# Running the chunked RWKV-7 recurrence on chunk transition matrices formed for eight chunks at a time

## The chip, the cores and the metric

The kernel runs on 1 core of one Trainium2 chip. The metric is the device time of one execution in microseconds (us), given as the median of several runs. One profiled execution, with its trace, is what the views below are read from.

## The reference

The reference is one layer of a hybrid encoder for 1024 tokens of width 1024: a projection of the normed input, three groups of heads on its columns (attention on a memory, a convolution module, a bidirectional RWKV-7 time mixing), an output projection, and a mixture of 16 experts, in float32. What matters here is the time mixing, 6 heads of 64, run forward and backward:

```python
def wkv7_scan(r, w, k, v, kk, a, reverse):
    def step(state, inp):
        r_t, w_t, k_t, v_t, kk_t, a_t = inp
        sa = jnp.einsum('bhij,bhj->bhi', state, -kk_t)
        state = (state * w_t[..., None, :]
                 + sa[..., :, None] * (kk_t * a_t)[..., None, :]
                 + v_t[..., :, None] * k_t[..., None, :])
        y_t = jnp.einsum('bhij,bhj->bhi', state, r_t)
        return state, y_t
    ...
    _, ys = lax.scan(step, state0, (r, w, k, v, kk, a), reverse=reverse)
```

## The kernel before

The scan is cut into chunks of C = 64 tokens. Two heads sit in the 128 partitions (`lo` and `hi`, 64 each), both directions d = 0, 1 go along together, and eight chunks (HC) make a unit, so there are six units u = 0 to 5: three pairs of heads, two halves of the sequence each. For each unit these generators run:

- `prep` (L775) forms, per direction, the decayed vectors: AR (from kk and r) and BK (from k and kk*a). BK is kept with zeros in the half of the partitions that belongs to the other head, so that a product over all 128 partitions is right; three VectorE operations and one of GpSimd of 64 partitions by 512 fill it (L823 to L826).
- `within` (L845) multiplies BK by AR inside each chunk (32 products of 128x128x128) and masks the result into AM with eight VectorE operations (L857).
- `invert` (L887) inverts the 64x64 triangles of all chunks of a unit at once: ScalarE copies blocks of AM into Ld (L895), VectorE turns them into Lt (L900), 31 dependent steps of two VectorE operations follow (L910, L911), then two turns, two scalings, and two rounds of small products with ScalarE copies (L926 to L949) give TT. Ld, Lt, Dt and their successors have one buffer each, so `invert` of the next unit starts when that of this one is through.
- `prep2` (L860) turns BK into BT and v into the first half of SV.
- `chain` (L954) is the recurrence. For a chunk it does, for both directions together: X = AM times v plus AR times the state (L969, L971), a VectorE copy to Xs (L973), SA = TT times Xs (L981), a VectorE and a ScalarE copy of the halves into SV (L982, L983), S1 = BT times SV (L988), and two VectorE operations that scale S1 and add the decayed old state `sps`, which GpSimd made (L991, L965). The outputs Y take two more products (L976, L996). A chunk is three steps of the generator, a unit 24.

The order of the work is written out by a planner: `run` (L224) steps through the chains as `mains`, and beside step i it steps other generators (`fills`) in proportion between two given steps: `within`, `inv`, `prep2` and `prep` of later units, `residual` (L1067, the output projection of the first five blocks, with its operands loaded from DRAM into one buffer each, `fo`), `finish`, and at the end `swap`, `out56` (L1176) and `partial` (L1168). Needs between them (name, count) force a generator to be stepped first. So `within` of unit u waits for steps 12 and 24 of chain u-2, `inv` for step 24 of chain u-2 and for `inv` of u-1, and chain u needs `inv` and `prep2` of u. Each engine runs its instructions in the order that comes out of this. After the chains the last normalisation, the router and the experts follow.

Of the kernel before, what the change touches and what calls it, by code (L numbers as in the profile page):

```python
# [20 lines left out]
P = 128  # L21
# [46 lines left out]
R_P1 = [26, 46]  # L68
# [3 lines left out]
R_W = [1, 2]  # L72
R_P2 = [4, 14]
R_INV = [-4, 22]
R_P = [4, 16]
R_PP = [-10, 8]
# [24 lines left out]
def hybrid_block_kernel(ctx: ExitStack, tc: tile.TileContext, x, xT, memT, memn, w_in, w_mk, w_mv, pcols,  # L101
# [47 lines left out]
    V.memset(bd64[64:128, 64:128], 1.0 / C)  # L149

# [503 lines left out]
    def early():  # L654
# [10 lines left out]

        Z["BK"] = [ge.tile([P, HC, 2, 2, C], F32, name=f"BK{d}") for d in range(2)]
        for bk in Z["BK"]:
            G.memset(bk[hi, :, 0], 0.0)
            G.memset(bk[lo, :, 1], 0.0)
# [13 lines left out]
    def late():  # L683
# [8 lines left out]
        for nm, shape in (("AR", [P, 2, HC, 2, C]), ("BT", [P, 2, HC, 2, C]), ("SV", [P, 2, HC, 2, C])):  # L692
            Z[nm + "b"] = gl.tile(shape, F32, name=nm + "b")
        g2 = pool("g2", stack=ph2b)
        for nm, shape in (("AR", [P, 2, HC, 2, C]), ("BT", [P, 2, HC, 2, C]), ("SV", [P, 2, HC, 2, C])):
            Z.setdefault(nm, []).append(g2.tile(shape, F32, name=nm + "a"))
            Z[nm].append(Z.pop(nm + "b"))
# [77 lines left out]
    def prep(p, k, g):  # L775
# [7 lines left out]
        for d in range(2):  # L783
# [60 lines left out]

    def within(g):  # L845

        for q, d in ((0, 0), (0, 1), (1, 0), (1, 1)):
            AM = g["AM", d, q] = Z["AM"][g["u"] % 2 * 4 + q * 2 + d]
            for h in range(2):
                ps = mm("A", shape=[P, 4, 2, C], name="psA", bufs=2)  # L850
                r_ = slice(h * 64, h * 64 + 64)
                for c in range(4):
                    cc = q * 4 + c
                    T.matmul(ps[:, c].rearrange("p a b -> p (a b)"),  # L854
                             lhsT=g["BK", d][:, cc, h].rearrange("p a b -> p (a b)"),
                             rhs=g["AR"][:, d, cc].rearrange("p a b -> p (a b)"), start=True, stop=True)
                V.tensor_tensor(AM[:, :, h], ps, mask[:, None].to_broadcast([P, 4, 2, C]), op=ALU.mult)  # L857
                yield

    def prep2(p, k, g):  # L860
        BT = g["BT"] = Z["BT"][g["u"] % 2]
        SV = g["SV"] = Z["SV"][g["u"] % 2]
        for d in range(2):
            n = k if d == 0 else 1 - k

            for h in range(2):
                ps = mm(shape=[P, HC, C])
                r_ = slice(h * 64, h * 64 + 64)
# [771 lines left out]
```

## Time and profile before

| | |
|---|---|
| median of 3 runs | 1480.16 us (1478.07 to 1490.92) |
| profiled execution: its own time | 1489.13 us |
| profiled execution: its span | 1487.2 us |
| mean granted TensorE clock | 0.927 |
| busy in the span: PE (TensorE matmul) | 1333.4 us, 90% |
| busy in the span: DVE (VectorE) | 1216.1 us, 82% |
| busy in the span: ACT (ScalarE) | 831.2 us, 56% |
| busy in the span: POOL (GpSimd) | 266.4 us, 18% |

How to read it: times are from the start of the span. Matmuls are pipelined, so a busy PE is not a PE at its peak. The chains run from about 381 to 802 us, the experts from about 880 us to the end. The shares above are means over stages with different limits, so the stage of the chains has to be looked at by itself.

### The profile page before, as it was taken

The numbers are of one execution on the slowest core, as the hardware profiler recorded it, in microseconds if no ns is written. First come the engines' busy times: TensorE is split into PE (matmuls) and PEld (weight loads), VectorE is DVE, ScalarE is ACT, GpSimd is POOL, SyncE is SP. The second block draws the span as 40 slices with busy tenths as digits, with TensorE's granted clock in tenths as the row PEclk, the third lists the DMA queues.
The fourth block names the chain that finished last, engine by engine and source line by source line (L and its number), as shares of the span: only waits on it lengthen the run. The fifth ranks groups of instructions, "written<-read, shape, count | busy, mean of one in ns | idle before, by whom it ended". The sixth has DMA issues, their size and how long they took to land.

```text
span 1487.2 us, 24329 instructions
## 1 busy us (share of the span) xinstructions
PE 1333.4 (90%) x9238; PEld 1069.4 (72%) x9238; DVE 1216.1 (82%) x2120; ACT 831.2 (56%) x1214; POOL 266.4 (18%) x238
## 2 busy tenths in 40 slices
PE   6888999997888889888999719999999999999996
PEld 5777667675777776767868618888888887887773
DVE  8899975699686869696833678999999988998886
ACT  4222574433535244434322418888888877887875
POOL 2233322532120312130221000100000110110010
PEclk9999899998898888888999859999999999999998
DMA  8212112422443533342473657999999999999985
GB/s 294 71 61 67 64 64 97 152 71 73 141 143 93 157 97 117 105 121 84 142 272 142 269 198 293 386 393 390 385 385 390 381 379 344 370 377 377 370 302 201
DMA packets 146100, 327.91 MB, mean 220 GB/s; under 512 B 9792, under 2 KB 64960, under 8 KB 145984
## 3 DMA queue, kind: packets, MB, share of 16 engines
q1 hardware_dynamic: 139360, 303.14, 55.6%
q0 software_dynamic: 6192, 22.55, 5.4%
q8 instruction: 72, 1.18, 0.3%
q10 hardware_dynamic: 432, 0.68, 0.1%
q14 instruction: 44, 0.36, 0.1%
HBM read 288.58 MB, written 37.75 MB: 219 GB/s over the span
## 4 chain that ended last, share of the span: by engine, by line
PE 60%; DVE 23%; DMA 6%; ACT 5%; issue 4%; POOL 1%; SPq 0%; POOLq 0%; DVEq 0%; ACTq 0%
PE mm L330 14%; PE mm L331 14%; PE mm L329 14%; DVE cv L517 3%; DVE dtmp L910 2%; DVE Dt L911 2%; DMA fo<-oT_d 2%; PE mm L1435 2%; ACT Ld L895 2%; DMA xk<-in_xT_dram 1%; PE mm L745 1%; PE psA L854 1%; DVE ewl L1354 1%; PE mm L1165 1%; PE mm L1575 1%
## 5 line engine op out<-in xcount | busy, mean ns | idle before, releaser
L1354 DVE SCALAR_TENSOR_TENSOR ewl<-eraw,pc,ewh 128x1024 fp32r<-128x1024 f32 x256 | 315.6, 1280 | 30.5 <-ACT ewh L1353 28.4
L1353 ACT ACTIVATE ewh<-eraw,pc 128x1024 fp32r<-128x1024 f32 x256 | 283.8, 1149 | 31.7 <-PE mm L331 25.7
L330 PE MATMUL mm<-ewl,xh 128*128 128x512 f32 x512 | 202.1, 395 | 3.2 <-DVE ewl L1354 3.0
L331 PE MATMUL mm<-ewh,xl 128*128 128x512 f32 x512 | 200.1, 391 | 0.0
L329 PE MATMUL mm<-ewh,xh 128*128 128x512 f32 x512 | 190.4, 397 | 2.5 <-ACT ewh L1353 2.5
L1350 DVE TENSOR_TENSOR ewl<-eraw,ewh 128x1024 fp32r<-128x1024 f32 x120 | 139.0, 1219 | 2.8 <-ACT ewh L1349 2.8
L329 PE MATMUL mm<-hh,wh 128*128 128x512 f32 x304 | 125.4, 413 | 9.6 <-ACT hh L310 9.6
L1349 ACT ACTIVATE ewh<-eraw 128x1024 fp32r<-128x1024 f32 x120 | 121.6, 1057 | 10.6 <-PE mm L331 9.5
L331 PE MATMUL mm<-hh,wl 128*128 128x512 f32 x304 | 125.5, 413 | 0.8 <-POOL wl L325 0.8
L330 PE MATMUL mm<-hl,wh 128*128 128x512 f32 x304 | 125.1, 412 | 0.9 <-DVE hl L311 0.9
L330 PEld LDWEIGHTS mm<-ewl,xh 128*128 128x128 f32 x512 | 96.6, 189 | 25.8 <-DVE ewl L1354 7.3
L329 PEld LDWEIGHTS mm<-ewh,xh 128*128 128x128 f32 x512 | 96.1, 188 | 23.2 <-ACT ewh L1353 4.2
L331 PEld LDWEIGHTS mm<-ewh,xl 128*128 128x128 f32 x512 | 96.3, 188 | 19.7 <-DVE xl L1438 0.2
L330 PE MATMUL mm<-ewl,fh 128*128 128x512 f32 x240 | 94.6, 394 | 0.3 <-DVE ewl L1350 0.2
L331 PE MATMUL mm<-ewh,fl 128*128 128x512 f32 x240 | 93.6, 390 | 0.0
L329 PE MATMUL mm<-ewh,fh 128*128 128x512 f32 x240 | 88.0, 390 | 0.0
L325 POOL TENSOR_TENSOR wl<-wraw,wh 128x512 fp32r<-128x512 f32 x38 | 58.7, 1548 | 124.5 <-ACT wh L324 83.6
L329 PEld LDWEIGHTS mm<-hh,wh 128*128 128x128 f32 x304 | 59.6, 196 | 25.4 <-ACT hh L310 9.6
L1472 POOL DMA_INDIRECT x_d<-ye,idx x15 | 25.9, 1724 | 283.3 <-ACT ye L1471 283.3
L1420 POOL DMA_INDIRECT xe<-h_d,idx x16 | 28.9, 1805 | 247.0 <-DVE gates L1418 182.3
L517 DVE SCALAR_TENSOR_TENSOR cv<-u,cw,cv 128x512 f32<-128x512 f32 (+1 forms) x87 | 71.5, 853 | 0.1
L330 PEld LDWEIGHTS mm<-hl,wh 128*128 128x128 f32 x304 | 59.1, 194 | 17.4 <-issue 2.7
(417 smaller groups left out, 2950.7 us busy)
## 6 DMA issues: line engine op xcount, KB each, us to landing
eraw<-in_w_eg_dram SPq DMA_DIRECT2D x64, 1024.0 KB, 7.9
eraw<-in_w_eu_dram SPq DMA_DIRECT2D x64, 1024.0 KB, 9.1
eraw<-in_w_ed_dram SPq DMA_DIRECT2D x64, 1024.0 KB, 7.4
fo<-oT_d SPq DMA_DIRECT2D x64, 320.0 KB, 3.9
wraw<-in_w_in_dram SPq DMA_DIRECT2D x38, 256.0 KB, 2.8
ld_k<-d_k SPq DMA_DIRECT2D x18, 256.0 KB, 3.1
ld_v<-d_v SPq DMA_DIRECT2D x18, 256.0 KB, 3.3
xk<-in_xT_dram SPq DMA_DIRECT2D x16, 256.0 KB, 4.7
```

Source lines behind the costliest of these rows:

```text
L325: G.tensor_sub(wl, raw, wh.bitcast(F32))
L329: T.matmul(ps, lhsT=lh, rhs=rh, start=first, stop=False)
L330: T.matmul(ps, lhsT=lh, rhs=rl, start=False, stop=False)
L331: T.matmul(ps, lhsT=ll, rhs=rh, start=False, stop=last)
L517: V.scalar_tensor_tensor(o[:, 0:ln], z, w, o[:, 0:ln], op0=ALU.mult, op1=ALU.add)
L895: A.copy(Ld[r_, :, c:c + 4].rearrange("p t c -> p c t"), g["AM", d, q][r_, :, h, 0, b * 32:b * 32 + 32])
L910: IE.tensor_tensor(tmp[:, sg, ts], lcol, drow, op=ALU.mult)
L911: IE.tensor_tensor(Dt[:, sg, ts], Dt[:, sg, ts], tmp[:, sg, ts], op=ALU.add)
L1349: A.activation(h, raw[a], AF.Copy)
L1350: V.tensor_sub(l, raw[a], h.bitcast(F32))
L1353: A.activation(h, raw[a], AF.Copy, scale=gain)
L1354: V.scalar_tensor_tensor(l, raw[a], gain, h.bitcast(F32), op0=ALU.mult, op1=ALU.subtract)
```

## The change

The state over a chunk is S1 = M S0 + own, with M = I plus a product that doesn't depend on the state. A new generator `solve` forms, for the eight chunks of a unit and both directions, M and the transposed output factor (both into AR) and the own part of the state (into the second half of BT), and the own corrections U (into the second half of SV). `chain` then does for a chunk the product M S0 on top of the own part, one VectorE operation that scales it, and the products of the outputs, which are put behind. `sps`, Xs, SA and the copies into SV are gone. BK loses its zeroed halves, so `within` and `prep2` use products of 64 partitions. The places of the fills and their needs are new. Two explicit orders (`edge`) keep products of different row halves that write one PSUM bank apart.

```diff
-R_P1 = [26, 46]
+R_P1 = [24, 33]
-R_W = [1, 2]
-R_P2 = [4, 14]
-R_INV = [-4, 22]
+R_W = [-10, -4]
+R_P2 = [0, 10]
+R_INV = [-7, 16]
+R_S = [11, 23]
+R_1 = {"within": [8, 12], "inv": [9, 20], "prep2": [9, 14], "solve": [17, 24]}
+R_S0 = [19, 23]
...
-            V.tensor_mul(BK[lo, :, 0, 0, :], kd[lo], cl[lo])
-            (G, V)[FL[7]].tensor_mul(BK[hi, :, 1, 1, :], kd[hi], cl[hi])
-            for r_, h, i in ((lo, 0, 1), (hi, 1, 0)):
-                V.scalar_tensor_tensor(BK[r_, :, h, i, :], sg[r_], -0.5, cl[r_], op0=ALU.mult, op1=ALU.mult)
+            V.tensor_mul(BK[:, :, 0, :], kd, cl)
+            V.scalar_tensor_tensor(BK[:, :, 1, :], sg, -0.5, cl, op0=ALU.mult, op1=ALU.mult)
...
+    HR = ((0, lo, hi), (1, hi, lo))
     def within(g):
...
+            for c in range(4):
+                cc = q * 4 + c
+                for i in range(2):
+                    for h, r_, w_ in HR:
+                        T.matmul(ps[h][w_ if i else r_, c].rearrange("p a b -> p (a b)"),
+                                 lhsT=g["BK", d][r_, cc, i], rhs=g["AR"][r_, d, cc].rearrange("p a b -> p (a b)"),
+                                 start=True, stop=True)
...
+    def solve(g):
+        AR, SV, BT = g["AR"], g["SV"], g["BT"]
+        U = SV[:, 1]
+        def each(tagp, f):
+            ps = mm(tagp, shape=[P, HC, C], name="psU")
+            for cc in range(HC):
+                for h, r_, w_ in HR:
+                    o, l, r = f(cc, h, r_, w_)
+                    T.matmul(ps[o, cc], lhsT=l, rhs=r, start=True, stop=True)
+            return ps
...
+        for d in range(2):
+            ps = each("mm", lambda cc, h, r_, w_: (w_, am(d, r_, cc, h, 0), SV[r_, 0, d, cc]))
+            A.copy(U[:, d], ps)
+            yield
+            ps = each("A", lambda cc, h, r_, w_: (w_, AR[r_, d, cc, 0, :], ident[r_, r_]))
+            A.copy(AR[:, d, :, 0, :], ps)
+            yield
+        TT = g["TT"].rearrange("p (d c) a b -> p d c (a b)", d=2)
+        for d in range(2):
+            ps = each("mm", lambda cc, h, r_, w_: (w_, TT[w_, d, cc], U[w_, d, cc]))
+            A.copy(U[:, d], ps)
+            yield
+            ps = each("A", lambda cc, h, r_, w_: (w_, TT[w_, d, cc], AR[w_, d, cc, 0, :]))
+            A.copy(AR[:, d, :, 0, :], ps)
+            yield
+        for d in range(2):
+            pm_ = each("mm", lambda cc, h, r_, w_: (r_, AR[w_, d, cc, 0, :], BT[w_, 1, d, cc]))
+            pr_ = each("A", lambda cc, h, r_, w_: (r_, AR[w_, d, cc, 0, :], am(d, w_, cc, h, 1)))
+            V.tensor_tensor(AR[:, d, :, 0, :], pm_, id2[:, None].to_broadcast([P, HC, C]), op=ALU.add)
+            yield
+            V.tensor_tensor(AR[:, d, :, 1, :], AR[:, d, :, 1, :], pr_, op=ALU.add)
+            yield
+        for d in range(2):
+            ps = each("mm", lambda cc, h, r_, w_: (r_, BT[w_, 1, d, cc], U[w_, d, cc]))
+            A.copy(BT[:, 1, d], ps)
             yield
...
+        def own(cc):
+            S1 = mm("cx", shape=[P, 2, C], name="psS", bufs=2)
+            for d in range(2):
+                for r_ in (lo, hi):
+                    T.matmul(S1[r_, d], lhsT=ident[r_, r_], rhs=BT[r_, 1, d, cc], start=(d == 0), stop=False)
+            for d in range(2):
+                for r_ in (lo, hi):
+                    T.matmul(S1[r_, d], lhsT=BT[r_, 0, d, cc], rhs=SV[r_, 0, d, cc], start=False, stop=False)
+            return S1
...
+        S1, St = own(0), []
         for cc in range(HC):
             S0 = state[0]
...
+            ms = [T.matmul(S1[r_, d], lhsT=AR[r_, d, cc, 0, :], rhs=S0[r_, d], start=False, stop=(d == 1)).ins
+                  for d in range(2) for r_ in (lo, hi)]
+            Sn = Z["sp"].tile([P, 2, C], F32, name="S0", bufs=4)
+            op = V.tensor_tensor(Sn, S1, pcs[:, :, cc:cc + 1].to_broadcast([P, 2, C]), op=ALU.mult)
             state[0] = Sn
+            if cc + 1 < HC:
+                S1 = own(cc + 1)
+            if cc == 0:
+                others = out_own(0, 1) + out_own(1, 1)
+            else:
...
+                    edge(lead, op.ins, mybir.DependencyClass.Sync)
...
+            for _ in range(3):
+                yield
...
+             "solve0": (solve(gs[0]), 14, *R_S0, [(0, "within0", None), (0, "prep20", None), (4, "inv0", None)]),
...
-        needs = [(1, f"inv{u}", None), (0, f"prep2{u}", None)]
+        needs = [(0, f"solve{u}", None)]
...
+            fills[f"within{u}"] = (within(gs[u]), 8, *at_(R_W if u > 1 else R_1["within"], u - 1), [(0, f"prep{u}", None), *after(u - 2, 0, 4)])
...
-            mains["swap"] = (swap(), 1, [(0, n, None) for n in ("res", "bon2", "pp2", "prep5", "within5", "inv5", "prep25")])
+            mains["swap"] = (swap(), 1, [(0, n, None) for n in ("res", "bon2", "pp2", "prep5", "within5", "solve5")])
```

In the parts left out `prep2` writes BT as two halves for both heads with 64x64 products against the identity (in place of transposes) and one full copy of v into SV; `out_own` and `out_state` hold the products of the outputs; `inv` of unit u waits for the first step of chain u-2, `prep2` for its step 19; chain S0 has four buffers.

## Rows read from the trace of the kernel before

**Rows 1.** Busy us (count) of PE, PEld, DVE, ACT, POOL; PEclk; DMA: stretches of `invert`.

```profile
316.40:355.20 38.80, 37.81 (x158) 29.23 (x156) 36.77 (x82) 8.25 (x10) 7.08 (x7) 1.00 0.11 41
398.30:456.60 58.30, 51.63 (x617) 43.36 (x617) 49.77 (x132) 17.57 (x34) 11.49 (x12) 0.91 0.46 136
470.40:529.50 59.10, 52.87 (x585) 43.02 (x586) 49.03 (x125) 17.92 (x34) 13.58 (x14) 0.79 0.42 127
529.50:546.90 17.40, 16.17 (x237) 13.70 (x237) 7.93 (x22) 10.99 (x24) 1.67 (x2) 0.83 0.24 70
546.90:610.90 64.00, 56.98 (x595) 45.62 (x594) 56.80 (x166) 22.81 (x43) 16.64 (x17) 0.81 0.39 118
628.80:680.90 52.10, 44.21 (x556) 34.87 (x548) 48.82 (x125) 17.18 (x35) 13.26 (x14) 0.90 0.40 119
696.40:736.90 40.50, 38.17 (x468) 32.63 (x468) 34.66 (x119) 11.16 (x21) 7.27 (x9) 0.84 0.47 141
747.90:840.00 92.10, 88.36 (x795) 71.59 (x794) 36.44 (x95) 23.06 (x45) 14.67 (x22) 0.93 0.53 206
```

**Rows 2.** Chain of waits from 456.6 to 747.9 us, shares by line.

```profile
by line: DVE dtmp L910 7.6%; DVE Dt L911 7.2%; DMA fo<-oT_d 7.0%; ACT Ld L895 6.1%; issue 4.7%; PE mm L329 4.3%; PE mm L331 3.9%; PE psS L988 3.4%; PE mm L745 3.3%; PE mm L330 3.2%; PE psA L854 2.9%; DMA fraw<-in_w_out_dram 2.4%; DVE BK L82
```

**Rows 3.** Timeline around one pause of `invert`, VectorE: start us, us, operation.

```profile
529.52 0.70 DVE L926 STREAM_TRANSPOSE D<-TT 128x512 f32<-128x512 f32 x1
...
546.89 1.24 DVE L900 STREAM_TRANSPOSE Lt<-Ld 128x1024 f32<-128x1024 f32 x1
```

**Rows 4.** Timeline in the same pause, ScalarE.

```profile
536.23 1.16 ACT L949 COPY TT<-mm 32x512 f32<-32x512 f32 x2 [0.85 <-PE mm L945]
...
538.95 3.34 ACT L895 COPY Ld<-AM 32x128 f32<-32x128 f32 x8
```

**Rows 5.** Groups by shape, 381 to 840 us: count | busy us, mean ns | idle before.

```profile
L895 ACT COPY Ld<-AM 32x128 f32<-32x128 f32 x80 | 32.4, 405 | 5.2 <-DVE AM L857 4.2
L857 DVE TENSOR_TENSOR AM<-psA,mask 128x512 f32<-128x512 f32 x39 | 26.6, 685 | 4.9 <-PE psA L854 4.5
...
L991 DVE SCALAR_TENSOR_TENSOR S<-psS,pcs,sps 128x64 f32<-128x64 f32 x96 | 24.7, 278 | 18.2 <-PE psS L988 17.7
...
L854 PE MATMUL psA<-ARb,BK 128*128 128x128 f32 x128 | 21.0, 299 | 2.0 <-DVE BK L826 1.6 <-DVE Dt L911 0.4
...
L973 DVE COPY Xs<-psX 128x128 f32<-128x128 f32 x48 | 13.7, 286 | 17.0 <-PE psX L971 15.6 <-PE psY L976 1.3
...
L826 DVE SCALAR_TENSOR_TENSOR BK<-sg,cl 64x512 f32<-64x512 f32 x16 | 12.4, 778 | 0.2
...
L823 DVE TENSOR_TENSOR BK<-ta,cl 64x512 f32<-64x512 f32 x9 | 9.1, 1012 | 0.0
...
L982 DVE COPY SVb<-psSA 64x128 f32<-64x128 f32 x24 | 7.1, 294 | 7.5 <-PE psSA L981 7.1
L871 ACT COPY BTb<-mm 128x512 f32<-128x512 f32 x12 | 7.0, 579 | 6.8 <-PE mm L870 6.8
```

**Rows 6.** Timeline of TensorE in one chunk of the last chain.

```profile
762.55 0.27 PE L976 MATMUL psY<-ARb,S 64*64 64x64 f32 x2
...
762.62 0.23 PE L971 MATMUL psX<-S,ARb 64*64 64x64 f32 x2
...
763.30 0.45 PE L981 MATMUL psSA<-Xs,TT 64*64 64x64 f32 x8 [0.30 <-DVE Xs L973]
763.68 0.49 PE L329 MATMUL mm<-wo,oh 128*128 128x512 f32 x1
```

**Rows 7.** Timeline of VectorE and GpSimd side by side in the third chain.

```profile
563.99 0.40 POOL L965 TENSOR_TENSOR sps<-S,pcs 128x128 f32<-128x128 f32 x1 [4.71 <-DVE S L991]
564.14 0.39 DVE L910 TENSOR_TENSOR dtmp<-Lt,Dt 128x120 f32<-128x120 f32 x1
...
571.42 1.27 POOL L824 TENSOR_TENSOR BK<-ta,cl 64x512 f32<-64x512 f32 x1 [7.03 <-DVE ta L819]
571.46 1.78 DVE L823 TENSOR_TENSOR BK<-ta,cl 64x512 f32<-64x512 f32 x1
```

More of the change, by code (lines that the diff above doesn't have):

```diff
@@ L664, in early @@
         Z["TT"] = [ge.tile([P, NCH, 2, 32], F32, name="TT0")]
[L666 to L669, printed above, removed]
+        Z["BK"] = [ge.tile([P, HC, 2, C], F32, name=f"BK{d}") for d in range(2)]
         Z["ep"] = ge.tile([P, HC, C + 1], F32, name="ep")
@@ L848, in within @@
             AM = g["AM", d, q] = Z["AM"][g["u"] % 2 * 4 + q * 2 + d]
-            for h in range(2):
[L850 to L857, printed above, removed]
+            ps = [mm("A", shape=[P, 4, 2, C], name="psA", bufs=2) for _ in range(2)]
+            for c in range(4):
[5 more added lines that the diff above has]
+                                 start=True, stop=True)
+            for h in range(2):
+                V.tensor_tensor(AM[:, :, h], ps[h], mask[:, None].to_broadcast([P, 4, 2, C]), op=ALU.mult)
                 yield
@@ new lines, in edge, with out_own @@
+        def edge(ins, other, cls):
+            tc.add_manual_dep(ins, other.name, mybir.DependencyInfo(cls, mybir.DependencyReason.DATA),
+                              reason="row tiles of one bank")
+        def out_own(d, i):
+            return [T.matmul(Y[d][r_, cc], lhsT=SV[w_ if i else r_, i, d, cc],
+                             rhs=g["AM", d, cc // 4][w_ if i else r_, cc % 4, h, 1, :],
+                             start=(i == 1 and cc == 0), stop=False).ins for cc in range(HC) for h, r_, w_ in HR]
@@ L966, in chain @@
-            X = mm("cx", shape=[P, 2, C], name="psX", bufs=2)
-            for d in range(2):
-                for h, r_, w_ in ((0, lo, hi), (1, hi, lo)):
-                    T.matmul(X[w_, d], lhsT=AM[d][r_, c4, h, 0, :], rhs=SV[r_, d, cc, h, :], start=True, stop=False)
-                for r_, w_ in ((lo, hi), (hi, lo)):
-                    T.matmul(X[w_, d], lhsT=AR[r_, d, cc, 0, :], rhs=S0[r_, d], start=False, stop=True)
-            Xs = Z["sp"].tile([P, 2, C], F32, name="Xs", bufs=2)
-            (A.copy if FL[3] else V.tensor_copy)(Xs, X)
@@ L974, in chain @@
-            for d in range(2):
-                for r_ in (lo, hi):
-                    T.matmul(Y[d][r_, cc], lhsT=S0[r_, d], rhs=AR[r_, d, cc, 1, :], start=True, stop=False)
-            yield
-            SA = mm("cx", shape=[P, 2, C], name="psSA", bufs=2)
-            for d in range(2):
-                for r_ in (hi, lo):
-                    T.matmul(SA[r_, d], lhsT=TT[r_, d, cc], rhs=Xs[r_, d], start=True, stop=True)
-            (A.copy if FL[4] else V.tensor_copy)(SV[hi, :, cc, 0, :], SA[hi])
@@ L983, in chain @@
-            (V.tensor_copy if FL[5] else A.copy)(SV[lo, :, cc, 1, :], SA[lo])
-            yield
-            S1 = mm("cx", shape=[P, 2, C], name="psS", bufs=2)
-            for d in range(2):
-                for h, r_ in ((0, lo), (1, hi)):
-                    T.matmul(S1[r_, d], lhsT=BT[:, d, cc, h, :], rhs=SV[:, d, cc, h, :], start=True, stop=True)
-            Sn = Z["sp"].tile([P, 2, C], F32, name="S0", bufs=3)
-            for d in range(2):
-                V.scalar_tensor_tensor(Sn[:, d], S1[:, d], pcs[:, d, cc:cc + 1], sps[:, d], op0=ALU.mult,
-                                       op1=ALU.add)
@@ L993, in chain @@
[L993 to L997 removed]
+            St.append(S0)
+            ms = [T.matmul(S1[r_, d], lhsT=AR[r_, d, cc, 0, :], rhs=S0[r_, d], start=False, stop=(d == 1)).ins
+                  for d in range(2) for r_ in (lo, hi)]
+            Sn = Z["sp"].tile([P, 2, C], F32, name="S0", bufs=4)
```

55 lines of the change are left out of this document (33 added, 22 removed).

## The prediction

> **What bounds the kernel now.** The page says PE 90% and DVE 82% busy, but these are means over the whole span, and the change touches only the stage of the chains (381 to 802 us) and the 38 us of leftovers behind it. I looked for what paces a unit there. In the chain of waits of that stage no line holds more than 8%: it hops between the two operations of an inversion step, the loads of `fo`, the copies to Ld, and matmuls [rows 2]. So I cut the stage at the two turns of `invert` that come once a unit, Lt and D. Between them lies a stretch in which 31 dependent steps run on VectorE; between D and the next Lt lies a pause [rows 3]. The stretches of units 1 to 5 take 58.3, 59.1, 64.0, 52.1 and 40.5 us, 274.0 in all, with VectorE busy for 239.1 of them, 87% [rows 1]. The pauses between the ends shown are 13.8, 17.4, 17.9 and 15.5 us, and 11.0 from the last D to 747.9, where TT of unit 5 is ready: 75.6 in all; VectorE is busy for 7.9 of the 17.4 in the pause shown. `invert` has one set of buffers, so stretch and pause follow each other strictly, and their sum, 350 us, is the stage. VectorE paces the stretches. The pause is a relay: D at 529.5, TT copied by 537.4, sixteen copies to Ld (0.405 us each, 6.5 in all [rows 5]) until Lt at 546.9 [rows 3, 4]. After 747.9 come 92.1 us in which PE is busy for 88.4 and VectorE for 36.4 [rows 1]: there TensorE is the bound.
>
> **The stretches.** The recurrence costs VectorE 13.7 us in Xs, 24.7 in the state, and twice 7.1 in SA (two buffers of SV, one shown): 52.6 for six units, 8.8 a unit [rows 5]. It becomes one operation a chunk from PSUM of 128x128. No row shows it; the Xs copy of that shape takes 0.286 us, the two halves of the state together 0.556. I take the first, since it is one instruction over the same elements: 2.3 us a unit, 4.4 at the other end, so 6.5 saved (4.4 at least). The stretches are 78% of the 350 us, so 5.1 of it falls into each, 25 us in five. BK costs VectorE one operation of 1.012 and two of 0.778 us a direction; it becomes two of full height, which I put at the 0.685 of the masked copy, the row of 128x512 [rows 5]: 2 x (2.57 - 1.37) = 2.4 a unit, for units 2 to 5, whose `prep` lies here, 9.6. `solve` adds four operations of 128x512 from PSUM, 4 x 0.685 = 2.7 a unit; its place is the second half of the chain before, half of which I put into the stretch: 1.4 x 5 = 7 (0 to 14). VectorE is relieved of 25 + 9.6 - 7 = 28 us; at 87% busy that is 32 us of time.
>
> The other part is idle time of VectorE, 35 us in the stretches. It stands at the head of its queue for Xs 17.0 us, for the state 18.2 and for SA 7.5 and more, 43 in 381 to 840 [rows 5], with the inversion steps queued behind each time. Three such hand-overs a chunk become one, with TensorE; but a queue that skips one wait meets the next (`fo` holds 7% of the chain of waits [rows 2]). I count 13 of the 35 us. Stretches: -45 (-20 if no wait goes and VectorE's added work all lies here, -60 if half of the idle goes too).
>
> GpSimd loses `sps` and its part of BK. The row where VectorE's part of BK lies beside GpSimd's shows 1.78 us, and a step beside `sps` its usual 0.39 [rows 7]; the mean of 1.012 above holds the first already. The Trainium skill, SBUF - State Buffer, section "Who interferes with whom", says that a VectorE operation with two SBUF inputs and a GpSimd operation that reads SBUF lock each other out whole, whoever starts first; the first pair agrees, the second shows no delay of VectorE. By that rule alone the eight `sps` of a unit, 0.4 us each, would give back up to 3 us more a unit, 16 in five; the sum goes by the rows.
>
> **The pauses.** Both halves of the relay stay, 7.9 and 6.5 us. `within` now runs a chain ahead, so no mask has to be waited for (the longer pauses hold some 3 us more than the relay). Against that, `solve` puts ten ScalarE copies of 128x512 into ScalarE's queue, 0.579 us each [rows 5], 5.8 a unit, and Ld's copies may stand behind them. 0 in all (-15 to +25).
>
> **TensorE.** A chain's own products stay 192 a unit. `prep2` splits each of its transposes into two products for the two halves of the rows, nothing in sum. `within` goes from 32 products of 128 rows to 64 of 64 rows. `solve` adds 224 products, 112 pairs. A pair alone takes 0.23 us, four pairs 0.45 [rows 6], so 0.07 each: 8 us a unit at the full clock (PEclk 1.00, 2.4 GHz), 16 where it is at 1.2. The stretches were granted 0.79 to 0.91, means of the two levels [rows 1]. In them PE shows busy 85 to 94%, which would leave no room; but a product of L854 lasts 0.299 us by its row, while 128 of them made PE busy for 21.0 us, 0.164 each [rows 5], so that a good part of "busy" is the tail of a pipeline that other products fill. I count nothing for it in the stretches, and the full 8 as a rival. Products of different quadrants run side by side (Y beside X [rows 6]), which would halve `within`, 5.2 us a unit; not counted. The Trainium skill, TensorEngine Tiling (Array Packing), section "Key Properties", says that a change of tiling mode drains TensorE. That speaks against 14 more bursts a unit of small products between the wide ones of `residual`. The last small burst starts at 763.30, ends at 763.75, and the wide product behind it starts at 763.68 [rows 6]: no drain longer than the last product's own length. The rule names no time; at the length of one small pair, 0.23 us, for each of two changes a burst, 14 bursts would cost 6 us a unit more, and rival (3) would be dearer by that.
>
> **Both ends.** `solve` now stands between `invert` and its chain. Where another inversion follows, VectorE has its stretch to run meanwhile; it is bare before chain 0 and for unit 5. Ten evacuations come behind TT, each a burst of 8 pairs (0.6 us) and a copy of 0.58 or an operation of 0.69, 1.2 us; the two directions overlap: 6 to 12 us. Before chain 0 `prep` of unit 1 can run beside it: +5 (0 to 12). For unit 5 the last chain and `swap`, and with it all of `out56`, wait: +10 (6 to 17). Behind it the 92.1 us of TensorE's work stay but for the idle 3.7 and some of the eight chunks' starts: -6 (-12 to 0).
>
> Sum: -45 + 0 + 5 + 10 - 6 = -36 on the profiled execution's 1489.1 us, 1453. That execution is 0.6% above the median; the same ratio on 1480.2 gives **1444 us**.
>
> **The rivals.** (1) VectorE gets so free that the stretches fall to the pace of those with no chain's hand-overs or little else in them, 38.8 us (unit 0) and 40.5 (unit 5) [rows 1]: 43 in the four middle ones saves 61, pauses of 12 us another 15: -61 - 15 + 15 - 6 = -67, 1413. For it: these two stretches exist. Against it: unit 0's had 95% of VectorE and no `finish` or `prep` beside it. (2) The gain is eaten: no idle goes (-20), each pause takes 4 of the 5.8 us of ScalarE's copies (+20), and the ends take +9: +9, 1489, and with half of the copies hidden -1, 1479. For it: the loads of `fo` have one buffer each and hold 7% already, and the step per chunk isn't short where own parts and outputs stand before it in TensorE's queue. Against it: the stretches are where VectorE is fullest. (3) Slower: TensorE is the bound in the stretches after all. Then VectorE's relief is worth nothing, and each unit pays 8 us (6 if `within` gets cheaper): 6 x 8 = 48 and the bare solves 15 less 6, +57, 1537; it is slower by over 1% from 1 us a unit on. For it: PE is busy 94% in the last stretch, and at least as much as VectorE in three others. Against it: the pipelined count above, and VectorE's idle time before the chain's operations, in which the products came late behind other work, not for want of TensorE's time alone. (4) That the change doesn't do what it says, a state over a chunk in one product and one operation, is not a case by itself: the code leaves it no other path; late products are in (2).
>
> **How the numbers follow.** Forecast 0.5, (1) 0.2, (2) 0.2, (3) 0.1. The range leaves out (3) and the far halves of (1) and (2), so 1405 to 1475. One per cent, 15 us, is about what a measurement of this kernel can tell from no change: faster than 1465 holds the forecast, (1) and a small part of (2), 0.77; the rest of (2) is 0.13 within; slower 0.10.
>
> **What would show it.** In the new profile: the time from Lt to D some 45 us for units 1 to 4, pauses still 13 to 18 us; VectorE's chain work one operation a chunk of about 0.29 us; its idle time before that operation under 15 us for 48; `solve` in the pauses on ScalarE; chain 5 starting at about 715 to 725 us. I'd be wrong if the stretches keep their length with VectorE at 75% (then TensorE or `fo`), if the pauses grow beyond 20 us (ScalarE's queue), or if the work behind unit 5 gets longer than 100 us.

## The result, and the profile after

The changed kernel takes 1545.3 us (median of 4 runs, 1543.7 to 1550.1), the kernel before 1483.3 beside it: ratio 1.042, 95% interval 1.036 to 1.047. It is slower by 62 us; 1444 was forecast. The profiled executions have spans of 1543.0 and 1487.2 us. Line numbers in this section are those of the changed kernel; `solve` is L892 to L936, all its products are L904.

The page's first rows say what moved: VectorE (DVE) is busy for 33 us less than before, TensorE (PE) for 41 us more, in 12886 instructions where there were 9238.

```profile
PE 1374.6 (89%) x12886; PEld 1127.1 (73%) x12886; DVE 1183.0 (77%) x1990; ACT 846.2 (55%) x1214; POOL 223.2 (14%) x174
```

The same cuts as in [rows 1], at Lt and D of each unit: busy us (count) of PE, PEld, DVE, ACT, POOL, then PEclk. The last row runs to the third addition of the last part of the output projection, from where both kernels run alike.

```profile
355.40:445.30 89.90, 70.98 (x1415) 61.82 (x1417) 41.82 (x80) 38.77 (x74) 11.36 (x8) 0.85 0.38 118
445.30:479.60 34.30, 17.17 (x428) 15.70 (x422) 31.60 (x87) 9.31 (x15) 2.70 (x1) 0.89 0.28 85
479.60:495.80 16.20, 13.85 (x234) 12.57 (x235) 2.05 (x5) 10.38 (x23) 0.00 (x0) 0.50 0.01 2
495.80:532.60 36.80, 31.04 (x763) 27.83 (x762) 34.33 (x91) 12.99 (x23) 5.10 (x3) 0.95 0.38 117
532.60:574.50 41.90, 38.63 (x839) 35.16 (x841) 16.75 (x32) 19.91 (x39) 2.99 (x2) 0.88 0.36 106
574.50:613.10 38.60, 35.00 (x602) 31.06 (x597) 34.00 (x115) 11.47 (x20) 3.81 (x3) 0.90 0.40 118
613.10:663.00 49.90, 46.16 (x853) 38.16 (x852) 27.18 (x52) 25.30 (x49) 8.65 (x6) 0.88 0.34 105
663.00:697.20 34.20, 29.90 (x596) 25.43 (x594) 32.20 (x84) 11.42 (x18) 5.08 (x3) 0.95 0.45 131
697.20:734.00 36.80, 33.34 (x812) 31.43 (x814) 19.95 (x35) 17.86 (x38) 2.86 (x2) 0.86 0.26 80
734.00:766.10 32.10, 27.45 (x526) 23.86 (x522) 28.93 (x91) 8.92 (x13) 3.81 (x3) 0.95 0.41 119
766.10:894.10 128.00, 120.00 (x1629) 104.31 (x1626) 39.79 (x99) 32.80 (x56) 16.76 (x18) 0.92 0.48 175
```

The two stretches of the kernel before that answer to the first and the last of these and are not in [rows 1]:

```profile
355.20:398.30 43.10, 29.77 (x363) 25.19 (x363) 31.36 (x53) 26.85 (x52) 12.06 (x9) 0.72 0.46 144
736.90:838.50 101.60, 97.30 (x1023) 79.58 (x1023) 39.21 (x109) 27.06 (x52) 17.97 (x26) 0.92 0.48 186
```

Added up, in us:

| part | before | after | difference | forecast | without `solve`'s products (below) |
|---|---|---|---|---|---|
| first D to second Lt | 43.1 | 89.9 | +46.8 | +5 | 78.1 |
| five stretches, Lt to D | 274.0 | 176.0 | -98.0 | -45 | 195.9 |
| four pauses, D to Lt | 64.6 | 144.8 | +80.2 | 0 | 91.3 |
| behind the last D | 101.6 | 128.0 | +26.4 | +4 | 114.0 |

So the stretches gave twice what was forecast, and everything between them took more than that back. In the stretches VectorE is busy 88 to 94% of the time; in the three long pauses TensorE is, 91 to 93%, while VectorE idles 46 to 60%. The two engines take turns. In the pause from 532.6 the chunk's operations (S), the next unit's masks (AM) and `solve`'s operations stand on VectorE in ones and twos, most of them after a wait for TensorE, which is busy for 38.6 us there (`solve`'s products have 14.8 of it, those of `residual` 14.4, of `within` 8.5); ScalarE's copies to Ld come in fours, each four behind a pair of masks. TT was copied 7.9 us after D before [rows 3, 4]; now it takes 23.

```profile
532.60 0.70 DVE L977 STREAM_TRANSPOSE D<-TT 128x512 f32<-128x512 f32 x1
...
547.82 0.69 DVE L862 TENSOR_TENSOR AM<-psA,mask 128x512 f32<-128x512 f32 x1 [3.24 <-PE psA L858]
...
555.28 0.29 DVE L1047 TENSOR_TENSOR S<-psS,pcs 128x128 f32<-128x128 f32 x1 [3.28 <-PE psS L1044]
560.92 1.29 DVE L862 TENSOR_TENSOR AM<-psA,mask 128x512 f32<-128x512 f32 x2 [5.35 <-PE psA L858]
...
574.52 1.25 DVE L951 STREAM_TRANSPOSE Lt<-Ld 128x1024 f32<-128x1024 f32 x1 [1.00 <-ACT Ld L946]
```

```profile
554.65 1.18 ACT L1000 COPY TT<-mm 32x512 f32<-32x512 f32 x2 [0.95 <-PE mm L996]
555.86 1.64 ACT L946 COPY Ld<-AM 32x128 f32<-32x128 f32 x4
...
561.65 1.67 ACT L946 COPY Ld<-AM 32x128 f32<-32x128 f32 x4 [0.98 <-DVE AM L862]
...
572.82 1.67 ACT L946 COPY Ld<-AM 32x128 f32<-32x128 f32 x4 [3.62 <-DVE AM L862]
```

In the groups by shape from 381 to 895 us the idle time ahead of the masks is 42.8 us, 4.9 before [rows 5]; the chunk's one operation (L1047) took 0.283 us and waits 17.1 us in all.

```profile
L946 ACT COPY Ld<-AM 32x128 f32<-32x128 f32 x80 | 32.5, 406 | 21.4 <-DVE AM L862 20.5
L862 DVE TENSOR_TENSOR AM<-psA,mask 128x512 f32<-128x512 f32 x40 | 26.5, 684 | 42.8 <-PE psA L858 42.8
L875 PE MATMUL mm<-ident,BK 64*64 64x64 f32 x640 | 25.3, 234 | 2.2 <-DVE fx L1158 1.6 <-ACT BTb L877 0.5
...
L1047 DVE TENSOR_TENSOR S<-psS,pcs 128x128 f32<-128x128 f32 x48 | 13.6, 283 | 17.1 <-PE psS L1044 17.1
```

What the forecast's price of a product missed stands in TensorE's timeline. A burst of 16 products of `solve` is 32 instructions, two a product, and takes 1.10 us; less the 0.22 of the last one that is 28 ns an instruction, 57 ns a product (the granted clock was 1.00 there). `own`'s four products with the identity (L1019) are eight instructions, and the next burst starts 0.23 us later, the same price.

```profile
500.76 1.10 PE L904 MATMUL psU<-AM,ARa 64*64 64x64 f32 x32
...
510.52 0.40 PE L1044 MATMUL psS<-S,ARa 64*64 64x64 f32 x8
510.75 0.40 PE L1019 MATMUL psS<-BTb,ident 64*64 64x64 f32 x8
510.98 0.40 PE L1022 MATMUL psS<-SVb,BTb 64*64 64x64 f32 x8
```

In [rows 6] "x8 0.45" was read as four pairs of products side by side; it is four products, eight instructions, so the prediction's 0.07 us was the price of one product and not of two. At 57 ns, `solve`'s 224 products are 12.8 us a unit, 77 in six.

### The profile page after: what moved, and what is told of

Its sections match the earlier page's. It is cut to its first block, busy times and chain, and to the rows that moved or that the text cites. A ratio compares the mean times of both kernels' runs of the same rounds, so it can differ in the third digit from the quotient of the medians.

```text
span 1543.0 us, 31355 instructions
## 1 busy us (share of the span) xinstructions
PE 1374.6 (89%) x12886; PEld 1127.1 (73%) x12886; DVE 1183.0 (77%) x1990; ACT 846.2 (55%) x1214; POOL 223.2 (14%) x174
## 4 chain that ended last, share of the span: by engine, by line
PE 58%; DVE 21%; issue 8%; DMA 6%; ACT 4%; POOL 2%; SPq 0%; POOLq 0%; DVEq 0%; ACTq 0%
PE mm L337 14%; PE mm L336 13%; PE mm L338 13%; DVE cv L524 3%; DVE dtmp L961 2%; PE psU L904 2%; DVE Dt L962 2%; PE mm L1506 2%; PE psA L858 1%; DVE ewl L1425 1%; DMA fo<-oT_d 1%; PE mm L1236 1%; PE mm L1646 1%; PE mm L615 1%; DMA fraw<-in_w_out_dram 1%
## 5 line engine op out<-in xcount | busy, mean ns | idle before, releaser
L1424 ACT ACTIVATE ewh<-eraw,pc 128x1024 fp32r<-128x1024 f32 x256 | 283.7, 1148 | 31.7 <-PE mm L338 26.4
L338 PEld LDWEIGHTS mm<-hh,wl 128*128 128x128 f32 x304 | 59.6, 196 | 17.5 <-POOL wl L332 3.7
L862 DVE TENSOR_TENSOR AM<-psA,mask 128x512 f32<-128x512 f32 x48 | 31.7, 684 | 47.1 <-PE psA L858 47.1
```

Source lines behind the costliest of these rows:

```text
L338: T.matmul(ps, lhsT=ll, rhs=rh, start=False, stop=last)
L862: V.tensor_tensor(AM[:, :, h], ps[h], mask[:, None].to_broadcast([P, 4, 2, C]), op=ALU.mult)
L1424: A.activation(h, raw[a], AF.Copy, scale=gain)
```

## The experiments

All ratios are to the kernel before, run beside each kernel on its chip; 0.010 is 15 us, and a difference between two of them is uncertain by some 10 us. The changed kernel's is 1.042.

**Order.** The first theory (O): the placements put `within` of the next unit into TensorE's queue among `solve`'s bursts, so the masks come late, and the second unit late too. The rival (T): the products themselves.

Masks first, for units 3 to 5:

```diff
+R_P3 = [0, 8]
+R_W3 = [-16, -10]
```

> The changed kernel with one placement moved, for units 3, 4 and 5 alone: prep at steps 0 to 8 of the chain two before (it stood at 4 to 16), and within at steps 8 to 14 of that chain (it stood at 14 to 20, among the bursts of solve of the unit before). The work is the same to the last instruction. Theory O (order: the long pauses come from within standing in TensorE's queue among and behind solve of the unit before, so that the next inversion's masks come late): the pauses ahead of Lt of units 3, 4 and 5, 41.9, 49.9 and 36.8 us in the changed kernel, fall to the 16 to 20 us that the pause ahead of unit 2 has, about -75 us; the mask operations move into the stretches, +5.5 us each at most; net -55 to -70 us, 1475 to 1490. Theory T (TensorE's time: the solve's 224 products a unit fill the time that TensorE had): the same products take the same time wherever they stand; what the pauses lose the stretches gain, and the time stays at 1530 to 1550.

Measured: ratio 1.044 (1.038 to 1.051), no gain. The pause ahead of Lt of unit 3 did shrink to 24.7 us, but the one ahead of unit 4 grew to 59.1, and TensorE is busy for 51.7 of it. The four pauses together lost 16 us, the five stretches gained 23.

Start first:

```diff
-R_P1 = [24, 33]
+R_P1 = [19, 24]
-R_1 = {"within": [8, 12], "inv": [9, 20], "prep2": [9, 14], "solve": [17, 24]}
+R_1 = {"within": [1, 3], "inv": [1, 16], "prep2": [3, 9], "solve": [11, 23]}
```

> The changed kernel with the placement of unit 1 alone moved: prep of unit 1 at steps 19 to 24 (it stood at 24 to 33), its within at steps 1 to 3 of chain 0 (8 to 12), its inversion at 1 to 16 (9 to 20), prep2 at 3 to 9 (9 to 14), solve at 11 to 23 (17 to 24). Theory O: Lt of unit 1, at 445.3 us in the changed kernel and at 398.3 before, comes at 400 to 415, and 30 to 45 us of that reach the end: 1500 to 1515. Theory T: the start was late because solve of unit 0 and chain 0 fill TensorE; Lt of unit 1 comes earlier, but chain 0 and what follows come later by about as much, and the end moves by less than 10 us: 1535 to 1550.

Measured: 1.037 (1.031 to 1.043). Lt of unit 1 came 16 us earlier, at 429.3, and the last D only 3 us earlier, at 763.0.

Both edits together:

> Both placements of the two kernels above at once. Theory O: the two gains add, since they lie in different stretches of time: -85 to -115 us from the changed kernel's 1545, so 1430 to 1460, below the kernel before (1483) and near the 1444 that was forecast. Theory T: TensorE's time is the same in all of them, 1525 to 1550.

Measured: 1.043 (1.036 to 1.050).

Solve last: `R_S = [18, 24]` in place of `[11, 23]`.

> The changed kernel with one number changed: solve of units 2 to 5 at steps 18 to 24 of the chain before (it stood at 11 to 23), so behind within of the next unit, which stays at 14 to 20. Theory O: the pauses ahead of Lt of units 3, 4 and 5 fall from 37 to 50 us to 18 to 25, as above; but the chain behind now waits for a solve that stands bare ahead of it while the inversion already runs, so half or more of it may come back in the chain: 1490 to 1540. Theory T: nothing changes but the order, 1535 to 1560.

Measured: 1.045 (1.038 to 1.052). Four placements, no gain beyond the uncertainty: theory O falls for this kernel. The work takes its time wherever it stands, as T has it.

**Price of a product, and whose time it is.** `solve`'s products twice:

```diff
-                    T.matmul(ps[o, cc], lhsT=l, rhs=r, start=True, stop=True)
+                    for _ in range(2):
+                        T.matmul(ps[o, cc], lhsT=l, rhs=r, start=True, stop=True)
```

> The changed kernel, every product of solve issued twice in a row into the same place (the second overwrites the first, the output is the same): 224 more products a unit, which are 448 more TensorE instructions, 2688 in all; no other engine gets work. At the 1.1 us that a burst of 16 products takes in the trace of the changed kernel they are 15.4 us a unit, 92 us in six. Theory T (TensorE's time is what the change cost): nearly all of it appears, +75 to +110 us from 1545. Rival L (the solve's cost is its relay of five bursts and copies, and TensorE has slack beside it): the extra products fill idle time of TensorE, +15 to +40 us.

Measured (two runs): 1.088 (1.077 to 1.099), 68 us above the changed kernel by the ratios, 77 by the medians. That is the lower edge of T's range and far outside L's. Then with the first of the two cut to 16 columns, `ps[o, cc, 0:16]` from `r[:, 0:16]`:

> As the kernel with solve's products issued twice, but the additional products have 16 columns where the product itself has 64, a quarter of the streamed columns and the same number of instructions. It asks what the price of a small product is made of. If the columns: a quarter of the price of the doubled kernel, +20 to +28 us. If the instruction (its weight load and start): the same price, +75 to +110 us.

Measured (two runs): 1.084 (1.076 to 1.093), 63 us by the ratios, 72 by the medians, not the 20 to 28 of a price by columns. The Trainium skill, TensorEngine Tiling (Array Packing), section "Instruction Overhead", says that a matmul of one column takes as long as one of 60; these two runs, with 16 and 64 columns, agree.

One of three products of `residual` left out, in the changed kernel and in the kernel before:

```diff
-                    mm3(ps, o[0][:, k], o[1][:, k], wh[:, k], wl[:, k], k == 0, k == 4)
+                    T.matmul(ps, lhsT=o[0][:, k], rhs=wh[:, k], start=k == 0, stop=False)
+                    T.matmul(ps, lhsT=o[1][:, k], rhs=wh[:, k], start=False, stop=k == 4)
```

> The changed kernel without one of the three products of residual's split multiplication in the stage of the chains (160 products of 128x256 left out, so the output lacks that correction term); nothing of the recurrence is touched and no other engine loses work. Their busy time is 49.7 us by the rows, some 21 us at 256 columns of pipelined time at the two clocks. Theory T: TensorE sets the pace of nearly every stretch, so 14 to 25 us come off 1545. Rival L: under 8 us.

> The kernel before with the same 160 products of residual left out (its output lacks that correction term). If VectorE paced its stretches, as the prediction took it, and TensorE had room there: under 8 us off the kernel before, ratio above 0.995. If TensorE was already the bound before the change (the prediction's third rival): 14 to 25 us off, ratio 0.983 to 0.991, as much as in the changed kernel.

Measured: the changed kernel 1.028 (1.020 to 1.036), 13 us by the medians, 21 by the ratios; the kernel before 1.006 (1.002 to 1.009), nothing gained. So time taken off TensorE shortens the changed kernel: there its busy time fell by 20 us. For the kernel before the run tells less than it seems to, because TensorE's time did not fall. From the first Lt to the last D, first in the kernel before, then without these products:

```profile
316.40:736.90 420.50, 365.24 (x4241) 299.39 (x4239) 335.86 (x865) 165.22 (x325) 85.75 (x88) 0.85 0.38 114
```

```profile
319.20:748.10 428.90, 365.60 (x4138) 296.21 (x4136) 336.03 (x875) 166.03 (x327) 84.99 (x89) 0.80 0.37 112
```

About 100 instructions fewer, the same busy time, and a granted clock of 0.80 where it was 0.85. Whether TensorE's time had a price in the kernel before stays open.

The counterpart on VectorE, 144 operations more in the chain of the changed kernel, and later, with 48 columns a direction in place of 64, in that of the kernel before:

```diff
+            for _ in range(3):
+                V.tensor_tensor(Z["more"], pcs[:, :, cc:cc + 1].to_broadcast([P, 2, C]),
+                                pcs[:, :, cc:cc + 1].to_broadcast([P, 2, C]), op=ALU.mult)
```

> The changed kernel with three more VectorE operations of the size of its chunk step (128x128, about 0.28 us each) behind each chunk step, into a tile that nothing reads: 144 operations, about 40 us of VectorE, about what the change took from it. It asks what VectorE's relief was worth. The prediction's own reckoning (28 us of VectorE less in the stretches are 32 us of time): +35 to +45 us. Theory T (VectorE paces only the stretches, and TensorE's queue holds the rest): +8 to +25 us. If VectorE's time is worth nothing: under 8 us.

> The kernel before with three more VectorE operations (2 x 48 elements on 128 partitions) behind each chunk step, 144 operations, 30 to 40 us of VectorE, into a tile that nothing reads; in the changed kernel the same kind of addition cost nothing. If VectorE paced the stretches of the kernel before, as the prediction read them: +20 to +40 us from 1488, ratio 1.013 to 1.027. If VectorE was not the pace there either, so that relieving it could not give what was forecast: under 8 us, ratio under 1.005.

Measured: VectorE's busy time rose by 34 us in the changed kernel, and the ratio is 1.038 (1.031 to 1.044): no price that these runs can tell. In the kernel before it rose by 25 us, and the ratio is 1.015 (1.008 to 1.021), 22 us; the five stretches grew by 13 us of it. So VectorE's time had a price before the change and has none after it, where TensorE's has one.

ScalarE, which the prediction suspected in the pauses: each of `solve`'s copies twice.

> The changed kernel with each of solve's ten ScalarE copies issued twice in a row (the second writes the same again): 60 more copies of 128x512, about 0.58 us each, 35 us of ScalarE. If the pauses are long because Ld's copies and the relay behind TT stand in ScalarE's queue, as the prediction named it: +20 to +35 us from 1545. If TensorE's time is the pace: under 8 us.

Measured: 1.045 (1.040 to 1.051), 5 us for 33 us of copies. It isn't ScalarE's queue. The second copies also lengthen the relay of bursts and copies in `solve` (TensorE is seen to wait for one, 1.4 us), so it isn't the length of that relay either, which the doubled products alone could not rule out.

**Fewer TensorE instructions.** K and B of a head as one weight of 128 columns in `within`, and one transpose for both in `prep2`:

```diff
-                for i in range(2):
-                    for h, r_, w_ in HR:
-                        T.matmul(ps[h][w_ if i else r_, c].rearrange("p a b -> p (a b)"),
-                                 lhsT=g["BK", d][r_, cc, i], rhs=g["AR"][r_, d, cc].rearrange("p a b -> p (a b)"),
-                                 start=True, stop=True)
+                for h, r_, w_ in HR:
+                    T.matmul(ps[h][:, c].rearrange("p a b -> p (a b)"),
+                             lhsT=both(g, d, cc, h), rhs=g["AR"][r_, d, cc].rearrange("p a b -> p (a b)"),
+                             start=True, stop=True)
...
+                    T.transpose(ps[:, cc, :], both(g, d, cc, h), ident[r_, r_])
```

> The changed kernel with two of its own parts undone on TensorE, the rest as it is: within loads K and B of one head as one weight of 128 columns (32 products a unit in place of 64, as before the change), and prep2 turns K and B of one head by one transpose (32 TensorE instructions in place of 128, as before). For that B K stands as K, B, K in three slots, which costs VectorE one half-height operation more a direction, about 1.4 us a unit. That is 64 + 96 = 160 TensorE instructions a unit less, 960 in all; doubling solve cost 77 us for 2688, 28.7 ns each. Theory T (TensorE's number of instructions is the price): -20 to -30 us from 1545, so 1515 to 1525. Rival L (relays and other engines): under 8 us.

Measured: 1.042 (1.035 to 1.050), nothing for 960 instructions less. A price per instruction, as I had put it, fails. The groups by shape show half of why: the transposes' busy time did fall against L875 above, to 16.7 us, but `within`'s products did not get cheaper with their number. Of those with ARb, the changed kernel's row and then this kernel's:

```profile
L858 PE MATMUL psA<-ARb,BK 64*64 64x128 f32 x256 | 16.7, 298 | 2.6 <-ACT ARa L916 2.1 <-ACT ARa L924 0.5
```

```profile
L879 PE MATMUL mm<-ident,BK 64*128 64x64 f32 x176 | 16.7, 249 | 2.8 <-DVE fx L1162 1.0 <-ACT ta L798 0.8 <-ACT BTa L880 0.6
L863 PE MATMUL psA<-ARb,BK 64*128 64x128 f32 x128 | 16.4, 299 | 1.2 <-DVE AM L867 1.2
```

Half as many instructions, the same busy time.

Three more such edits at once:

```diff
+                        T.matmul(ps[w_, c].rearrange("p a b -> p (a b)"), lhsT=TT[w_, d, cc],
+                                 rhs=UA[w_, d, cc].rearrange("p a b -> p (a b)"), start=True, stop=True)
...
+                    T.transpose(ps[lo, c, 1], AR[hi, d, cc, 0], ident[hi, hi])
...
+                T.transpose(ps[lo, c, :], vt[lo, c * C:(c + 1) * C], ident[lo, lo])
...
+            T.matmul(S1, lhsT=ident, rhs=UA[:, :, cc, 1], start=True, stop=False)
```

> The kernel with one weight for K and B, and three more parts done with fewer TensorE instructions, the output the same: solve takes U and the transposed A through TT in one product of 128 columns (32 products a unit less, 64 instructions), those transposes that land on the lower half of the rows are single transposes (16 instructions less for A and 16 for v), and the chain adds its own part by one product of 128 rows with the identity in place of four a chunk (24 products, 48 instructions less). Another 144 a unit, 864 in all. Copies and VectorE's work stay. Theory T: another -20 to -27 us, 1488 to 1505, level with the kernel before (about 1485 to 1490) or up to 1.3% above. Rival L: under 8 us from the kernel with one weight alone.

Measured: 1.106 (1.099 to 1.113), 96 us above the kernel with one weight, where 20 to 27 less were expected. The timeline shows a part of it: turning v, products (L890) and single transposes (L891) alternate, and each pair takes 0.43 us, so eight chunks take 3.4.

```profile
572.23 0.32 PE L890 MATMUL mm<-ident,vr 64*64 64x64 f32 x2
572.48 0.24 PE L891 MATMUL mm<-ident,vr 64*64 64x64 f32 x1
572.65 0.33 PE L890 MATMUL mm<-ident,vr 64*64 64x64 f32 x2
```

In the changed kernel the same eight chunks are one burst of 1.10 us:

```profile
529.06 1.10 PE L888 MATMUL mm<-ident,vr 64*64 64x64 f32 x32
```

That is 2.3 us more for each of 12 such bursts, 28 us; the clock was 1.00 in both rows. `solve`'s transposes are mixed in the same way. The rest of the 96 us isn't told apart: the granted clock of the stage was 0.79 here and 0.89 in the changed kernel, and the edit also leaves TT one buffer where it had two.

With the two placements of the first runs (unit 1 early, masks of units 3 to 5 early) added:

> The kernel with fewer TensorE instructions in the placements of the two placement runs (prep and within of unit 1 early; prep and within of units 3 to 5 early). If TensorE still paces every stretch, the order gives nothing here either: within 15 us of the kernel with fewer instructions. If TensorE now has room, the order that gave nothing before gives part of its 75 to 115 us: 20 to 60 us below that kernel, and below the kernel before.

Measured: 1.089 (1.083 to 1.095), 26 us below the kernel with fewer instructions, far above the kernel before; why the order helps here and not in the changed kernel was not followed up.

The fourth edit alone, the whole identity:

```diff
-            for d in range(2):
-                for r_ in (lo, hi):
-                    T.matmul(S1[r_, d], lhsT=ident[r_, r_], rhs=BT[r_, 1, d, cc], start=(d == 0), stop=False)
+            T.matmul(S1, lhsT=ident, rhs=BT[:, 1, :, cc], start=True, stop=False)
```

> The changed kernel with one edit in the chain: the four products a chunk with the identity (64x64 each, eight TensorE instructions) become one product of 128 rows with the whole identity (two instructions), the output the same; 288 TensorE instructions less in all. The kernel with fewer instructions had this edit among others and was 108 us slower. Theory N (a price per instruction, 28.7 ns): -8 us from 1545. Theory D (the change between products on a quadrant and products on the whole array is what costs): in that kernel's trace the 128-row product's two instructions and the one before them took 148, 213 and 205 ns from start to start, where instructions on quadrants start 29 ns apart in the mean, so some 0.57 us a chunk against 0.25: 48 x 0.3 = +10 to +20 us.

Measured: 1.046 (1.041 to 1.052), 7 us above the changed kernel, which is within the uncertainty: N's 8 us less are not met, D's 10 to 20 more are not shown by the time. The timeline speaks for D. In one chunk, at a clock of 1.00 in both, where the changed kernel above takes 0.46 us from M's products (L1044) over the identity's to the next burst, this kernel (L1042, L1017, L1020) takes 0.74:

```profile
508.93 0.40 PE L1042 MATMUL psS<-S,ARa 64*64 64x64 f32 x8
509.25 0.49 PE L1017 MATMUL psS<-BTb,ident 128*128 128x128 f32 x2
509.67 0.27 PE L1020 MATMUL psS<-SVb,BTb 64*64 64x64 f32 x2
```

**Is `solve` the whole loss?** Its bursts are left out, its copies and operations stay, from SBUF:

```diff
-            ps = each("mm", lambda cc, h, r_, w_: (w_, am(d, r_, cc, h, 0), SV[r_, 0, d, cc]))
-            A.copy(U[:, d], ps)
+            A.activation(U[:, d], SV[:, 0, d], AF.Copy, scale=0.0)
```

> The changed kernel without the 224 products of solve (its 14 bursts a unit are left out; its ten copies and four operations stay, of the same size, from SBUF, with a scale of zero, so the state is not the reference's). Everything else of the change stays: BK's two operations, the chunk's one product and one operation, the placements, the start. Theory T': the changed kernel is slower by TensorE's time for solve's products and by nothing else of size; doubling them cost 77 us, 57 ns a product, so leaving them out gives at least as much, with the waits for them 77 to 100 us: 1445 to 1468, some 20 to 40 us below the kernel before, which is what the prediction expected of the change without a price for TensorE. Rival W (the changed order and the inversion that starts late in the first unit cost most of it): 1485 to 1520.

Measured: 1.003 (1.000 to 1.006): 58 us less than the changed kernel by the ratios, 54 by the medians, but no less than the kernel before. The time, 1491 us, lies in W's range and misses that of T'. `solve`'s products are still about the whole difference to the kernel before, as T' has it; but they give back 54 to 58 us and not 77 or more, and the rest of the change is worth nothing, where T' wanted 20 to 40 us. One thing that differs beside them is the granted clock, 0.85 from the first Lt to the end of the last row and 0.89 with the products; what that took off the gain was not tested. The cuts of this kernel (last column of the table above) say where: the stretches still gain 78 us, the way to the second Lt costs 35 more than before, the pauses 27 more, the end 12 more.

```profile
354.20:432.30 78.10, 62.51 (x993) 52.38 (x995) 43.70 (x80) 39.02 (x75) 11.42 (x8) 0.76 0.46 135
...
595.80:629.50 33.70, 29.28 (x426) 23.56 (x428) 22.37 (x45) 22.07 (x43) 7.30 (x5) 0.85 0.44 134
...
719.50:833.50 114.00, 104.83 (x1140) 89.14 (x1139) 38.87 (x97) 30.93 (x53) 16.78 (x18) 0.91 0.53 192
```

The two placements again, without `solve`'s products:

> The kernel without solve's products (its output is not the reference's) and with unit 1 placed earlier, as in the run that moved the start alone (prep at steps 19 to 24, within at 1 to 3 of chain 0, its inversion at 1 to 16, solve's copies at 11 to 23). With solve's products there, that placement gave nothing. Without them Lt of unit 1 still came at 432.3 us, against 398.3 in the kernel before, and the gaps between D and Lt hold 27 us more than before, and what the stretches won was lost there. Theory P (besides solve's products it is the placements that lose what the stretches gain; solve's products hid that, since they filled TensorE wherever the work stood): 20 to 35 us come off 1491, so 1455 to 1470. Theory Q (the rest is TensorE's time too, the other products' and the residual's with their loads): under 8 us.

> The kernel without solve's products (its output is not the reference's) in both earlier placements, of unit 1 and of prep and within of units 3 to 5. Theory P: 30 to 60 us come off 1491, so 1430 to 1460, about the time that was forecast for the whole change. Theory Q: within 10 us of 1491.

Measured: 0.994 (0.990 to 0.997) and 1.000 (0.996 to 1.003). The start is worth 14 us here, below the 20 to 35 of P; masks first loses 10 of it. So the placement of the start is part of what the rest of the change loses. The run with both is the nearest to the forecast's own picture: its five stretches add up to 230.6 us, 43 less than before (45 were forecast), and its four pauses to 74.3, 10 more. What was won there goes at the ends, 14 us more up to the second Lt and 19 more behind the last D. One part of the latter can be seen: `residual` has 45 products left there, 15 in the kernel before. For the rest no run tells which engine or load it is, and it stays open.

## Why the prediction was wrong, point by point

- **What bounds the kernel before**: right as far as it was tested. VectorE had the price (22 us for 25 us added); that TensorE had none isn't shown, since leaving out products didn't lower its busy time.
- **The stretches, -45**: direction right, size short by half, -98. The relief was as forecast where it was worked out: 0.283 us for the chunk's operation (0.286 forecast), idle ahead of it 17.1 us (under 15). BK's first operation took 1.36 us in the mean (0.69 to 1.79), not 0.685. But a stretch that ends earlier only hands over to a pause, which the sum took as fixed.
- **TensorE, "8 us a unit ... nothing for it in the stretches"**: the step that failed, in size and in place. A product costs 57 ns, a "pair" of the prediction was one product's two instructions, so `solve` is 12.8 us a unit; and it doesn't lie under VectorE's stretches: only some 600 of its 2688 instructions stand there, the others in the pauses and at both ends. Doubling it costs 68 to 77 us, leaving it out gives 54 to 58, about the whole distance to the kernel before (62).
- **The pauses, "no mask has to be waited for"**: failed, +80. The sign that was named, pauses beyond 20 us, came, but not from ScalarE's queue. `within` of the next unit is placed in the same steps as `solve`, and the masks wait 42.8 us for TensorE. The order alone isn't the cause, as the placement runs show; nor are ScalarE's copies, as their doubling shows. 54 of the 80 us go when `solve`'s products are left out.
- **prep2, "nothing in sum"**: the products against the identity are 128 instructions a unit where the transposes were 32; undoing that, with `within`'s edit, gave nothing, so the step did no harm that a run can tell.
- **Both ends, +5, +10, -6**: failed, +46.8 and +26.4. Without `solve`'s products 12 us of the first go and 14 of the second; the earlier placement moved the second Lt by 16 us in the changed kernel, and a gain of 14 us reached the end only without these products.
- **Rival (3)**, TensorE is the bound, relief worth nothing, +57 and 1537: the nearest to what happened, at a chance of 0.1. That its number is so close is partly luck: it took 8 us a unit for 12.8, and it put the bound into the stretches, which did get shorter. Its argument for itself, PE busy for as much as VectorE in three stretches, was waved off with the pipeline; the right question was how much a unit's TensorE work could grow before the pauses and the ends, where VectorE covers nothing, are full.

## What to carry to other kernels

A step that trades a serial operation on one engine for many small products on another should be priced first by what an instruction costs from start to start in a burst (28 ns here, two instructions to a float32 product); doubling the products then shows whether that time is free. Where two engines take turns in one loop, relief of the one that paces half of it is lost if the other gets longer: sum both halves for both engines. Fewer instructions were no gain here where they broke up uniform bursts. And when work is taken off TensorE to see what it is worth, look at the granted clock and the busy time of that run: in the kernel before, the clock fell with it, and TensorE was busy for as long as ever.

## What the runs showed of the hardware

- A float32 product of 64 rows and 64 columns costs 57 ns from start to start at a granted clock of 1.00, as two instructions. Products added with 16 columns cost as much as with 64 (63 against 68 us for 1344). The two heads' products of such a burst stand on different quadrants; no row has a burst on one quadrant to compare.
- The granted clock differed between kernels: 0.85 before and 0.80 with 160 of `residual`'s products left out (first Lt to last D), 0.89 in the changed kernel and 0.85 without `solve`'s products (first Lt to the end of the last row). Why is not shown.
- Breaking up a burst costs: one 128-row product between bursts on quadrants takes 0.28 us more a chunk than the four small ones that it replaces; product and transpose in turn, both of 64 by 64, take 0.43 us where a pair of products in a uniform burst takes 0.14 (1.10 us for eight). The Trainium skill, TensorEngine Tiling (Array Packing), section "Key Properties", says that switching the mode drains TensorE. The prediction took the gap in [rows 6] as showing no drain, but at 28 ns an instruction those rows show a gap: the wide product starts 0.38 us after the first of the eight small instructions (0.38 and 0.37 in the two chunks before it), where above a burst of the same shape follows after 0.23. A cost at such a switch is shown, then; that it is a drain is not, and the product and transpose of one shape show that a change of shape is not the only thing that costs. In the changed kernel itself most of `solve`'s bursts are uniform, 32 instructions each.
